# Attention by pairs of heads in the front of a two-layer model, with the front's steps dealt anew

## The chip, the core and the metric

The kernel runs on one NeuronCore of a Trainium2 chip. Its engines are TensorE (PE in the rows, with PEld for its weight loads), VectorE (DVE), ScalarE (ACT), GpSimd (POOL) and SyncE (SP), whose queue issues the DMAs. Each engine takes its own instructions in order; semaphores tie them together. The metric is the device time of one launch in microseconds.

## The reference, cut to what matters

One sequence of 256 tokens, 1024 channels, 16 heads of 64 channels. Layer 0 is a recurrent time mix and a dense feed-forward; layer 1 is attention and a mixture of eight experts. With one block of 256 keys the attention has no other blocks to select, so it is plain causal attention:

```python
q = _heads(x @ w_q).transpose(0, 2, 1, 3)
s_own = jnp.einsum('bhqd,bhkd->bhqk', q_c, k_own).astype(jnp.float32) * scale
s_own = jnp.where(k_pos[None, :] <= q_pos[:, None], s_own, -jnp.inf)
p = jax.nn.softmax(jnp.concatenate([s_sel, s_own], axis=-1), axis=-1)
o = ... + jnp.einsum('bhqk,bhkd->bhqd', p_own.astype(v_own.dtype), v_own)
return (o @ w_o).astype(x.dtype)
...
logits = (x @ router).astype(jnp.float32)
top_logits, top_idx = lax.top_k(logits, TOP_K_EXPERTS)
for e in range(N_EXPERTS):
    out = out + gates[..., e:e + 1] * swiglu(x, w_gate[e], w_up[e], w_down[e])
```

## The kernel before

The program has two parts. `front` does everything up to the router: the projections of the time mix, its chunked scan in four units (two halves of the channels by two tiles of 128 tokens), the output projection, the dense feed-forward, the projections to keys, queries and values, attention, its output projection and the choice of experts. `moe` then streams the weights of the eight experts from HBM, 2 MB at a time, through nine places in SBUF, and multiplies them with the tokens gathered for each expert.

Inside `front` the work is written as generators ("chains"), each a row of steps that ends at a `yield`. A string of letters, `ORDER`, says which chain makes its next step; the instructions land on their engines' queues in exactly that order, for PE, DVE, ACT, POOL and SP alike. Chains `a` to `d` are the units of the scan, `v` is `project_out` (values, keys and queries, then the output projection), `h`, `i`, `j`, `k` are four attention chains, `n` is `heads_out`, and `A` fetches expert weights ahead.

Weights of `front` arrive as 1 MB raw blocks. ACT casts each half block to a rounded high part (line 287) and DVE subtracts it to get a low part (line 288); a product is then three matmuls, high by high, high by low, low by high (lines 317 to 319; 1075 to 1078 for keys and queries).

Attention before takes one head at a time. `heads(i)` makes the heads 4·grp + i. Queries and keys lie with channels on partitions, two heads to a tile, so a head is one half of the 128 rows. Per head PE makes the scores of query tile 0 against key tile 0 (line 1134, 128 columns) and of query tile 1 against both key tiles (line 1136, 256 columns), each with a stationary side of 64 rows, and after each adds the causal mask by a 128-column bf16 matmul with an identity (lines 1135, 1137). An fp32 matmul is two instructions in the trace. DVE takes the row maxima (1140 to 1142), ACT the exponentials with their sums (1145). PE transposes the three 128x128 pieces of P (1150), DVE copies them out for even heads and ACT for odd ones (1153), and PE multiplies with the transposed P as the stationary side and 64 columns of values moving (1157 to 1159). `heads_out` takes four heads at a time: it divides by the sums (1169, 1171), transposes the result to channel-major with four PE transposes (1181) and splits it into high and low for the output projection. The PSUM tag `sc` has six banks, `mm` two.

Of the kernel before, what the change touches and what calls it, by code (L numbers as in the profile page):

```python
# [21 lines left out]
N = 64  # L22
# [159 lines left out]
def load_ln(g, i):  # L182
# [16 lines left out]
    "pXPmPXPXPmPPmpPXmmPpppppPpmppmpsppmPpspsPpppPssppmpPspPspppmPsPmppppGpppmmppmppvpmPGGPpPppXmmPGGmGPp"  # L199
    "mmpppPpmpPpGPGppspGmGaaaPasaOPsapaappPGOGOppppsPpspppppOapPbpObaaOpsaappaGOpaapbPpaPaappaaeasPppabaP"  # L200
    "basbbObpPpaaOappaGbaPpObapaabdpapbaadbpbbbpEddppabadPPpOdEcbbOEbapbEbaOdEdbbcddpcbddcdpbdddppccbpdEb"
    "dpdpbbpdcbcbpbbsdaadbabdcdbaadbabbdbbcbcdbbcdEccddbddeEdeeEeeeEldeecEeceEeEceeccEeeEEecddeeecEeeEcde"
    "edcdEccdceeccedeccdccceeceedcecEedEecedcecELemEccEeeceeccecLLedLeLcleLLlllLlLlllLlLlllllLllLLlllllll"
    "llLLelLLleLllllllLlllllllLlLllLlElLLlllllLLLlLLlalLlLlLlllllLlLlllcLLllLllLlllLLlLLllllllLlLLLllLLll"
    "LLlLLllllLLlllllllLlLlLllLLLlOLLllLllLLlllllllLllLlLLllLllLllLlLLllllllLlllLLlLlllllllLlLLlllLlLLlll"
    "LllllLLLlllLLlllllLLlLLLlllLlllLLlllLLLlLlLlLLLlblLLLWlllllLllWyyllyylWyyylyllyWWWyyyllWllzLWxvzvvzv"
    "zzvzzvzvzvzzvzvvvWvWvvWAvvWvvWWvvWWvvvWvyvWvvvWvWWWWvvvhkiWhAWhPjkvvvvAvWjWvivjhikhjiWjkkWWAkvnvWzWv"
    "AWhvvvvvijhkijnhhWjjikAjAWkkiWiWjWvvhinvvrvvvWvkhjknihhhiWnWikhkjAvijWvvWvWvkjihWWnijknvrvnvvvnvvWWv"
    "fvvvGuvvvAfvkffdvfAvfWfvivgvfruguAfgAArwuugwgugwjwAuuwgwftwwgtugggxfAqqAtqhwtqqqtAttxA"
# [24 lines left out]
def front(es, g, split, zH, zL, res):  # L234
# [774 lines left out]
    qT, kT, V, oT, av, sums = {}, {}, {}, {}, {}, {}  # L1009
# [30 lines left out]
    def project_out():  # L1040
# [51 lines left out]
        for j in range(2):  # L1092
            for kc in range(4):
                yield from W.need(kc * 512)
                yield "o%d" % (kc // 2)
                for tt in range(NT):
                    oH, oL = oT[0]
                    product(po[tt, j], oH[:, kc, tsl(tt)], oL[:, kc, tsl(tt)], *W.cols(kc * 512, 512), kc == 0, False)
                yield
        ws = {}  # L1100
        for tt in range(NT):
            for j in range(2):
                for kc in range(4):
# [5 lines left out]
                    yield "o%d" % (2 + kc // 2)  # L1109
# [8 lines left out]
    def heads(i):  # L1118

        for grp in range(4):  # L1120
            h = 4 * grp + i
            hp, s = divmod(h, 2)
            j, c = divmod(hp, 4)
            if i == 0:
                yield "at"
                av[grp] = bank("sc", (128, NT, 4, N))
                sums[grp] = g.small.tile([128, NT, 4], F32, name="sums", tag="sums")
                steps.post("av%d" % grp)
            yield "av%d" % grp
# [9 lines left out]
            st = g.small.tile([128, 4], F32, name="ast", tag="ast", bufs=4)  # L1139
            nc.vector.tensor_reduce(st[:, 0:1], sc[:, 0:128], AX, OP.max)  # L1140
            nc.vector.tensor_reduce(st[:, 1:2], sc[:, 128:384], AX, OP.max)
            nc.vector.tensor_scalar(st[:, 2:4], st[:, 0:2], -0.125, None, op0=OP.mult)
            P_ = att("P", (128, 384), 4)
            for tt, cs in enumerate((slice(0, 128), slice(128, 384))):
                nc.scalar.activation(P_[:, cs], sc[:, cs], AF.Exp, bias=st[:, 2 + tt:3 + tt], scale=0.125,
                                     accum_out=sums[grp][:, tt, i:i + 1])
            yield
            pt = bank("sc", (128, 384))
            for n in range(3):
                nc.tensor.transpose(pt[:, n * 128:(n + 1) * 128], P_[:, n * 128:(n + 1) * 128], g.ident)  # L1150
            PT = att("PT", (128, 384), 4)
# [4 lines left out]
            hs = slice(h % 8 * N, h % 8 * N + N)  # L1156
# [3 lines left out]
            steps.post("av%d.%d" % (grp, i))  # L1160
            yield

    def heads_out():

        for grp in range(4):
            for i in range(4):
                yield "av%d.%d" % (grp, i)
# [691 lines left out]
```

## Time and profile before

| | us |
|---|---|
| median of 3 runs | 1445.87 (1444.23 to 1451.18) |
| the profiled execution | 1449.14 |
| its span, first to last instruction | 1447.3 |
| first matmul on expert weights | 612.88 |
| PE busy over the span | 1338.2 (92%) |
| DVE busy | 779.7 (54%) |
| ACT busy | 380.8 (26%) |

The rows below come from the profiled execution. A window row gives, for a stretch of the span, how long each engine was busy (instructions in brackets), the clock that TensorE was granted (1.00 is 2.4 GHz, 0.50 is 1.2 GHz), the share of time that the 16 DMA engines were busy, and GB/s. A timeline row gives start, duration, engine, line, operation, out<-in and shapes; since matmuls overlap, the time that one costs its engine is the distance to the next row's start, not its duration.

### The profile page before, as it was taken

What the parts mean: (1) busy time and instruction counts of PE and PEld (TensorE: products, weight loads), DVE (VectorE), ACT (ScalarE), POOL (GpSimd) and SP (SyncE); (2) the same over time, 40 slices, a digit from 0 to 9 for tenths busy, and PEclk for the clock granted to TensorE, in tenths of its full rate; (3) what the DMA queues carried; (4) which work ended last, traced back from release to release, by engine and by line L of the source; (5) the groups of instructions that cost most, each with busy time, mean ns of one, the idle gap of its engine ahead of it and who ended that gap; (6) DMA issues with size and microseconds to landing.
All of it is one profiled execution on the core that took longest, in us unless ns stands there. A gap on an engine that the chain in (4) does not pass through costs nothing. (4 is left out here: it accounts for less than half of the span.)

```text
span 1447.3 us, 25902 instructions
## 1 busy us (share of the span) xinstructions
PE 1338.2 (92%) x10935; PEld 756.1 (52%) x10935; DVE 779.7 (54%) x1884; ACT 380.8 (26%) x678; POOL 10.4 (1%) x32
## 2 busy tenths in 40 slices
PE   7999998899999999899987999997999999998874
PEld 5776876678878987733332334332443343332221
DVE  8777888664558344744643433543432433544445
ACT  5666655453433343301110100110100110100100
POOL 1000000000000000000000000000000000000000
PEclk9999999999999988799999999999999999999997
DMA  6533153565554553779999999999999999999993
GB/s 219 207 134 107 37 188 135 179 241 188 204 204 164 214 204 118 291 310 425 423 425 424 422 426 425 423 424 422 425 426 423 425 400 406 403 425 421 424 425 159
DMA packets 49876, 446.58 MB, mean 309 GB/s; under 512 B 5792, under 2 KB 5920, under 8 KB 11840
## 3 DMA queue, kind: packets, MB, share of 16 engines
q1 hardware_dynamic: 49728, 444.42, 76.0%
q8 instruction: 115, 1.88, 0.5%
q14 instruction: 33, 0.27, 0.1%
HBM read 443.35 MB, written 1.05 MB: 307 GB/s over the span
## 5 line engine op out<-in xcount | busy, mean ns | idle before, releaser
L1460 PE MATMUL gu<-raw,x 128*64 128x512 f32 x1216 | 279.1, 604 | 27.4 <-DMA raw<-wm 22.8
L1498 DVE STREAM_TRANSPOSE t<-s 32x64 f32<-32x64 f32 (+1 forms) x896 | 241.4, 269 | 15.3
L288 DVE TENSOR_TENSOR w<-raw,w 128x1024 fp32r<-128x1024 f32 x140 | 168.2, 1221 | 87.5 <-ACT w L287 87.0
L1471 PE MATMUL y<-raw,t 128*64 128x512 f32 x880 | 200.7, 594 | 11.8 <-DMA raw<-wm 11.8
L1483 DVE TENSOR_TENSOR s<-s,gu 64x512 f32<-64x512 f32 x56 | 38.0, 679 | 298.7 <-ACT s L1482 298.7
L1460 PEld LDWEIGHTS gu<-raw,x 128*64 128x64 f32 x1216 | 88.8, 138 | 196.9 <-issue 154.8
L287 ACT CAST w<-raw 128x1024 fp32r<-128x1024 f32 x140 | 144.2, 1050 | 94.4 <-DMA raw<-wd 44.1
L1460 PE MATMUL gu<-half,x 128*64 128x512 f32 x576 | 134.9, 615 | 12.9 <-DMA half<-wm 9.7
L1471 PEld LDWEIGHTS y<-raw,t 128*64 128x64 f32 x880 | 65.6, 137 | 133.7 <-issue 125.3
L1482 ACT ACTIVATE s<-gu 64x512 f32<-64x512 f32 x56 | 33.2, 593 | 370.0 <-PE gu L1460 370.0
L1460 PEld LDWEIGHTS gu<-half,x 128*64 128x64 f32 x576 | 42.9, 141 | 94.1 <-issue 85.8
L1489 ACT ACTIVATE s<-gx 64x256 f32<-64x256 f32 x56 | 21.0, 375 | 266.9 <-PE gx L1465 144.8
L1490 DVE TENSOR_TENSOR s<-s,gx 64x256 f32<-64x256 f32 x56 | 23.8, 425 | 103.5 <-ACT s L1489 102.0
L317 PE MATMUL sc<-w,h 128*128 128x512 f32 (+1 forms) x176 | 66.8, 380 | 0.0
L318 PE MATMUL sc<-w,h 128*128 128x512 f32 (+1 forms) x176 | 66.5, 378 | 0.1
L319 PE MATMUL sc<-w,l 128*128 128x512 f32 (+1 forms) x176 | 66.1, 375 | 0.0
L1465 PE MATMUL gx<-raw,x 128*32 128x256 f32 x832 | 47.6, 380 | 1.1 <-DVE t L1498 1.1
L1465 PEld LDWEIGHTS gx<-raw,x 128*32 128x32 f32 x832 | 26.1, 110 | 27.0 <-issue 11.7
L1477 PE MATMUL yx<-raw,t 128*32 128x256 f32 x672 | 40.2, 379 | 0.0
L318 PEld LDWEIGHTS sc<-w,h 128*128 128x128 f32 x176 | 33.3, 189 | 7.2 <-DVE w L288 0.8
L317 PEld LDWEIGHTS sc<-w,h 128*128 128x128 f32 x176 | 33.3, 189 | 6.5
L319 PEld LDWEIGHTS sc<-w,l 128*128 128x128 f32 x176 | 33.3, 189 | 6.5
(405 smaller groups left out, 1903.3 us busy)
## 6 DMA issues: line engine op xcount, KB each, us to landing
raw<-wm SPq DMA_DIRECT2D x112, 2048.0 KB, 24.6
half<-wm SPq DMA_DIRECT2D x74, 1024.0 KB, 24.5
raw<-wd SPq DMA_DIRECT2D x72, 1024.0 KB, 4.9
raw<-wm SPq DMA_DIRECT2D x38, 1024.0 KB, 30.8
vec<-vecs SPq DMA_DIRECT2D x20, 256.0 KB, 5.6
ln<-vecs SPq DMA_DIRECT2D x8, 512.0 KB, 7.0
x<-xT SPq DMA_DIRECT2D x4, 256.0 KB, 5.6
raw<-wd SPq DMA_DIRECT2D x2, 512.0 KB, 5.4
```

What stands on the lines that cost most here:

```text
L287: nc.scalar.copy(wh, raws[n - 1][:, cs])
L288: nc.vector.tensor_sub(wl, raws[n - 1][:, cs], f32(wh))
L317: nc.tensor.matmul(o, ah, bh, start=start, stop=False)
L318: nc.tensor.matmul(o, ah, bl, start=False, stop=False)
L319: nc.tensor.matmul(o, al, bh, start=False, stop=stop)
L1460: nc.tensor.matmul(a.pg[64 * m:64 * m + 64], a.x[:, kc, 0:MAIN], w[m], start=kc == 0, stop=kc == KC - 1)
L1465: nc.tensor.matmul(a.px[32 * q:32 * q + 32], a.x[:, kc, MAIN:CAP], w[q // 2][:, q % 2 * 256:q % 2 * 256 + 256], start=kc == 0, stop=kc == ...
L1471: nc.tensor.matmul(a.y[64 * n:64 * n + 64], a.t[:, kt, 0:MAIN], w[:, n * 512:n * 512 + 512], start=a.j == 0 and kt == 0, stop=a.j == NJ - ...
L1477: nc.tensor.matmul(a.yx[32 * q:32 * q + 32], a.t[:, kt, MAIN:CAP], w[:, q * 256:q * 256 + 256], start=a.j == 0 and kt == 0, stop=a.j == NJ ...
L1482: nc.scalar.activation(a.s[0:64], a.pg[64:128], AF.Silu)
L1483: nc.vector.tensor_mul(a.s[0:64], a.s[0:64], a.pg[0:64])
L1498: nc.vector.transpose(a.t[32 * b:32 * b + 32, k:k + n // 128, c:c + 32], src[:, b])
```

## The change

Attention is made by pairs of heads. A chain makes the pairs `i` and `4 + i`; a pair is one whole tile of queries and keys. Its two heads get a PSUM bank each for their scores. A bf16 matmul of 384 columns first writes the mask into each bank; then the two heads' score matmuls follow in turn, one on the upper 64 rows of the array, the other on the lower 64. DVE divides P by its sums before the transposes (a reciprocal and four multiplications by a column for each pair). All copies of the transposed P are ACT's. The second product has the values as the stationary side, 64 columns for each head, and the transposed P moving (256 columns for key tile 0, 128 for key tile 1); its two heads write the two halves of one bank's partitions, channel-major already, so `heads_out` and its transposes are gone and each pair is split by itself. The output projection waits for each pair instead of each four heads. `ORDER` is a new string for the whole of `front`. The expert part is the same.

```diff
-                yield "o%d" % (kc // 2)
+                yield "o%d" % kc
...
-                    yield "o%d" % (2 + kc // 2)
+                    yield "o%d" % (4 + kc)
...
-        for grp in range(4):
-            h = 4 * grp + i
-            hp, s = divmod(h, 2)
+        for hp in (i, 4 + i):
             j, c = divmod(hp, 4)
...
-            q_, k_ = qT[j][HF[s], c], kT[j][HF[s], c]
-            sc = bank("sc", (128, 384))
-            nc.tensor.matmul(sc[:, 0:128], q_[:, 0:128], k_[:, 0:128], start=True, stop=False)
-            nc.tensor.matmul(sc[:, 0:128], g.identb, g.cmask, start=False, stop=True)
-            nc.tensor.matmul(sc[:, 128:384], q_[:, 128:256], k_, start=True, stop=False, skip_group_check=True)
-            nc.tensor.matmul(sc[:, 256:384], g.identb, g.cmask, start=False, stop=True, skip_group_check=True)
+            q_, k_ = (t[j][:, c] for t in (qT, kT))
+            sc = [bank("sc", (128, 384)) for _ in range(2)]
+            for s in range(2):
+                nc.tensor.matmul(sc[s], g.identb, g.cmask, start=True, stop=True)
+            for cs, qs, ks in ((slice(0, 128), slice(0, 128), slice(0, 128)), (slice(128, 384), slice(128, 256), slice(0, 256))):
+                for s in range(2):
+                    nc.tensor.matmul(sc[s][:, cs], q_[HF[s], qs], k_[HF[s], ks], start=False, stop=True,
+                                     skip_group_check=True)
...
+            nc.vector.reciprocal(st[:, 0], st[:, 2])
+            for s in range(2):
+                for tt, cs in enumerate(cols):
+                    nc.vector.tensor_scalar(P_[s][:, cs], P_[s][:, cs], st[:, 0, s, tt:tt + 1], None, op0=OP.mult)
...
-            eng = nc.scalar.copy if s else nc.vector.tensor_copy
-            eng(PT, pt)
+                nc.scalar.copy(PT[s], pt)
...
-            nc.tensor.matmul(av[grp][:, 0, i], PT[:, 0:128], V[j][:, 0, hs], start=True, stop=True)
-            nc.tensor.matmul(av[grp][:, 1, i], PT[:, 128:256], V[j][:, 0, hs], start=True, stop=False)
-            nc.tensor.matmul(av[grp][:, 1, i], PT[:, 256:384], V[j][:, 1, hs], start=False, stop=True)
+            av = bank("sc", (128, 256))
+            for kt, qs, ps in ((0, slice(0, 256), slice(0, 256)), (1, slice(128, 256), slice(256, 384))):
+                for s in range(2):
+                    v_ = V[j][:, kt, (2 * c + s) * N:(2 * c + s) * N + N]
+                    nc.tensor.matmul(av[HF[s], qs], v_, PT[s][:, ps], start=kt == 0, stop=True, skip_group_check=True)
...
-            rs = g.small.tile([128, NT, 4], F32, name="rs", tag="rs")
-            nc.vector.reciprocal(rs, sums[grp])
-            o = att("o", (128, NT, 4, N), 2)
-            nc.vector.tensor_mul(o, av[grp], rs[:, :, :, None].to_broadcast([128, NT, 4, N]))
...
-            for c in range(2):
-                for tt in range(NT):
-                    nc.tensor.transpose(p[:, c, tt], o[:, tt, 2 * c:2 * c + 2].rearrange("p h n -> p (h n)"), g.ident)
-            split_to(nc, *(t[:, c] for t in oT[grp // 2]), p.rearrange("p c t n -> p c (t n)"))
+            split_to(nc, *(t[:, c] for t in oT[j]), av)
```

Of the table of letters, the end (attention and router) before and now:

```diff
-    "AWhvvvvvijhkijnhhWjjikAjAWkkiWiWjWvvhinvvrvvvWvkhjknihhhiWnWikhkjAvijWvvWvWvkjihWWnijknvrvnvvvnvvWWv"
+    "vvjWrWWAivWvvkiikjikkjkvWvjvkjvvkvrkWWWkjkhivvjWikAhWihhkAWWvvWvvvviAWhhivhiijhiAiWvjvvjvWvfvvvvfffh"
```

PE in the middle of attention, where one head's scores are followed by another head's second product. Before:

```order
L1134 MATMUL sc<-K,Q 128x128
L1135 LDWEIGHTS identb
L1135 MATMUL sc<-cmask,identb 128x128
L1136 MATMUL sc<-K,Q 128x256
L1137 LDWEIGHTS identb
L1137 MATMUL sc<-cmask,identb 128x128
L1157 MATMUL sc<-V,PT 128x64
L1158 MATMUL sc<-V,PT 128x64
L1159 MATMUL sc<-V,PT 128x64
```

Now, the transposes of two pairs, then a pair's masks and scores, then a pair's second product:

```order
L1158 MATMUL sc<-ident,P 128x128 x12
L1129 LDWEIGHTS identb
L1129 MATMUL sc<-cmask,identb 128x384
L1129 LDWEIGHTS identb
L1129 MATMUL sc<-cmask,identb 128x384
L1132 MATMUL sc<-K,Q 128x128 x2
L1132 MATMUL sc<-K,Q 128x256 x2
L1167 MATMUL sc<-PT,V 64x256 x2
L1167 MATMUL sc<-PT,V 64x128 x2
```

The masks moved ahead of the scores, the two heads of a pair stand side by side, and the second product has 64 output partitions with 256 or 128 columns for each instruction.

PE at the end of attention, before the last output projections; `oH` is the high part of the attention's output, `w` the projection's weights. Before:

```order
L1150 MATMUL sc<-ident,P 128x128 x9
L1157 MATMUL sc<-V,PT 128x64
L1158 MATMUL sc<-V,PT 128x64
L1159 MATMUL sc<-V,PT 128x64
L1181 MATMUL sc<-ident,o 128x128 x4
L1157 MATMUL sc<-V,PT 128x64
```

Now:

```order
L1158 MATMUL sc<-ident,P 128x128 x6
L317 MATMUL mm<-w,oH 128x512
L318 MATMUL mm<-w,oH 128x512
L319 MATMUL mm<-w,oL 128x512
L317 MATMUL sc<-w,oH 128x512
L318 MATMUL sc<-w,oH 128x512
L319 MATMUL sc<-w,oL 128x512
L1167 MATMUL sc<-PT,V 64x256 x2
L1167 MATMUL sc<-PT,V 64x128 x2
L1158 MATMUL sc<-ident,P 128x128 x6
L1167 MATMUL sc<-PT,V 64x256 x2
L1167 MATMUL sc<-PT,V 64x128 x2
```

Six projection matmuls now stand between one pair's transposes and its second product, and a second product of another pair behind the last transposes.

ACT in the scan stage, where sigmoid (463, 481) and exponential (511, 528) need different tables. Before:

```order
L526 ACTIVATE X<-GK 128x512
L528 ACT_TABLE_LOAD
L528 ACTIVATE AR<-AR 128x512
L529 ACTIVATE GK<-sc 128x512
L530 ACTIVATE AR<-sc 128x512
L583 COPY bT<-sc 128x512
L105 CAST zH<-xm 128x512
L583 COPY bT<-sc 128x512
L511 ACTIVATE pch<-sc 128x4x2
L463 ACT_TABLE_LOAD
L463 ACTIVATE h<-sc 128x512
```

Now:

```order
L583 COPY bT<-sc 128x512 x2
L511 ACT_TABLE_LOAD
L511 ACTIVATE pch<-sc 128x4x2
L481 ACT_TABLE_LOAD
L481 ACTIVATE sg<-sc 128x160
L287 CAST w<-raw 128x1024 x2
L486 COPY sgA<-sc 128x128
L487 COPY sgB<-sc 32x128
L526 ACTIVATE X<-GK 128x512
L528 ACT_TABLE_LOAD
```

The sigmoids moved between exponentials; over the whole program there are twelve table loads instead of ten.

## Rows read from the trace of the kernel before

**Rows 1.** The page, 40 slices: TensorE's granted clock in tenths.

```profile
PEclk9999999999999988799999999999999999999997
```

**Rows 2.** Windows by stage: PE, PEld, DVE, ACT, POOL busy; clock, DMA share, GB/s.

```profile
72.00:288.00 216.00, 196.36 (x4073) 154.56 (x4072) 168.90 (x329) 122.87 (x227) 2.15 (x3) 0.96 0.37 129
...
464.00:592.00 128.00, 128.00 (x771) 108.35 (x770) 62.09 (x121) 49.19 (x109) 0.00 (x0) 0.89 0.50 191
...
612.00:628.00 16.00, 14.96 (x60) 5.39 (x62) 6.74 (x25) 3.36 (x5) 0.00 (x0) 0.83 0.42 158
628.00:1180.00 552.00, 520.60 (x3574) 203.52 (x3572) 239.45 (x747) 56.76 (x127) 0.00 (x0) 1.00 1.01 423
1180.00:1260.00 80.00, 79.44 (x672) 31.37 (x670) 32.92 (x104) 8.19 (x18) 0.00 (x0) 1.00 0.97 395
```

**Rows 3.** Timeline of PE: start, us, engine; the first matmuls on expert weights.

```profile
612.88 5.39 PE L1460 MATMUL gu<-raw,x 128*64 128x512 f32 x14 [0.97 <-ACT x L1348]
```

**Rows 4.** Timeline of PE: one head's scores and second product, full clock.

```profile
510.48 0.48 PE L1134 MATMUL sc<-K,Q 64*128 64x128 f32 x2
510.90 0.23 PE L1135 MATMUL sc<-cmask,identb 128*128 128x128 bf16 x1
511.06 0.70 PE L1136 MATMUL sc<-K,Q 64*128 64x256 f32 x2
511.69 0.23 PE L1137 MATMUL sc<-cmask,identb 128*128 128x128 bf16 x1
511.75 0.39 PE L1157 MATMUL sc<-V,PT 128*128 128x64 f32 x2
...
512.51 0.48 PE L1134 MATMUL sc<-K,Q 64*128 64x128 f32 x2
```

**Rows 5.** Timeline of PE: the same of another head at half clock.

```profile
534.20 0.79 PE L1134 MATMUL sc<-K,Q 64*128 64x128 f32 x2
...
536.37 0.64 PE L1157 MATMUL sc<-V,PT 128*128 128x64 f32 x2
...
537.79 0.79 PE L1134 MATMUL sc<-K,Q 64*128 64x128 f32 x2
```

**Rows 6.** Windows as in Rows 2: the stretches of half clock within attention.

```profile
491.00:498.00 7.00, 7.00 (x28) 5.27 (x28) 3.08 (x8) 3.85 (x14) 0.00 (x0) 0.51 0.43 157
...
532.00:542.00 10.00, 10.00 (x36) 7.34 (x36) 4.33 (x10) 4.09 (x11) 0.00 (x0) 0.50 0.31 108
...
559.50:569.00 9.50, 9.50 (x27) 6.14 (x26) 6.50 (x15) 4.97 (x15) 0.00 (x0) 0.50 0.32 113
```

**Rows 7.** Timeline of PE: tiles on two row halves (L759), two column halves (L1460).

```profile
212.41 0.68 PE L759 MATMUL sc<-D,FQ 64*64 64x64 f32 x16
212.93 0.75 PE L642 MATMUL sc<-P,LT 64*64 64x64 f32 x30
...
1413.28 3.65 PE L1460 MATMUL gu<-raw,x 128*64 128x512 f32 x16 [1.09 <-DMA raw<-wm]
1416.76 0.60 PE L1471 MATMUL y<-raw,t 128*64 128x512 f32 x2
```

**Rows 8.** Timeline of PE: four transposes of the attention's output, full clock.

```profile
575.13 0.60 PE L1181 MATMUL sc<-ident,o 128*128 128x128 f32 x4
575.58 0.33 PE L1157 MATMUL sc<-V,PT 128*128 128x64 f32 x2
```

**Rows 9.** Groups by line and shape: count, busy us, mean ns, idle before.

```profile
L1153 DVE COPY PT<-sc 128x384 f32<-128x384 f32 x8 | 4.4, 554 | 6.8 <-PE sc L1150 6.8
L1153 ACT COPY PT<-sc 128x384 f32<-128x384 f32 x8 | 3.7, 481 | 9.4 <-PE sc L1150 9.4
L1171 DVE TENSOR_TENSOR o<-sc,rs 128x512 f32<-128x512 f32 x4 | 2.8, 692 | 0.3
L1145 ACT ACT_TABLE_LOAD x1 | 1.3, 1283 | 2.2 <-DVE ast L1142 2.2
...
L1373 DVE TENSOR_SCALAR G<-slots,pos,sel 128x96 fp32r<-128x96 f32 x16 | 4.6, 327 | 0.3
```

**Rows 10.** Waits of PE up to 440 us: us in total, times, longest.

```profile
PE sc L871 <- DVE h L154: 5.3, 2, 4.9
```

More of the change, by code (lines that the diff above doesn't have):

```diff
@@ L1008, in front @@
     at = []
-    qT, kT, V, oT, av, sums = {}, {}, {}, {}, {}, {}
+    qT, kT, V, oT = {}, {}, {}, {}
     def rooms():
@@ L1163, in heads_out @@
[L1163 to L1167, printed above, removed]
-            rs = g.small.tile([128, NT, 4], F32, name="rs", tag="rs")
-            nc.vector.reciprocal(rs, sums[grp])
-            o = att("o", (128, NT, 4, N), 2)
-            nc.vector.tensor_mul(o, av[grp], rs[:, :, :, None].to_broadcast([128, NT, 4, N]))
-            yield
-            if grp == 0:
+            q_, k_ = (t[j][:, c] for t in (qT, kT))
+            sc = [bank("sc", (128, 384)) for _ in range(2)]
@@ new lines, in heads @@
+            for s in range(2):
[4 more added lines that the diff above has]
+                                     skip_group_check=True)
+            yield
+            st = g.small.tile([128, 3, 2, NT], F32, name="ast", tag="ast", bufs=4)
@@ new lines, in heads @@
+            cols = (slice(0, 128), slice(128, 384))
+            for s in range(2):
+                for tt, cs in enumerate(cols):
+                    nc.vector.tensor_reduce(st[:, 0, s, tt:tt + 1], sc[s][:, cs], AX, OP.max)
+            nc.vector.tensor_scalar(st[:, 1], st[:, 0], -0.125, None, op0=OP.mult)
+            yield
+            P_ = [att("P", (128, 384), 4) for _ in range(2)]
+            for s in range(2):
+                for tt, cs in enumerate(cols):
+                    nc.scalar.activation(P_[s][:, cs], sc[s][:, cs], AF.Exp, bias=st[:, 1, s, tt:tt + 1], scale=0.125,
+                                         accum_out=st[:, 2, s, tt:tt + 1])
@@ new lines, in heads @@
+            yield
+            nc.vector.reciprocal(st[:, 0], st[:, 2])
+            for s in range(2):
+                for tt, cs in enumerate(cols):
+                    nc.vector.tensor_scalar(P_[s][:, cs], P_[s][:, cs], st[:, 0, s, tt:tt + 1], None, op0=OP.mult)
+            yield
+            PT = []
+            for s in range(2):
+                pt = bank("sc", (128, 384))
+                for n in range(3):
+                    nc.tensor.transpose(pt[:, n * 128:(n + 1) * 128], P_[s][:, n * 128:(n + 1) * 128], g.ident)
+                PT.append(att("PT", (128, 384), 4))
+                nc.scalar.copy(PT[s], pt)
+                yield
@@ L1174, in heads_out @@
+            yield "V%d" % j
+            av = bank("sc", (128, 256))
+            for kt, qs, ps in ((0, slice(0, 256), slice(0, 256)), (1, slice(128, 256), slice(256, 384))):
+                for s in range(2):
+                    v_ = V[j][:, kt, (2 * c + s) * N:(2 * c + s) * N + N]
+                    nc.tensor.matmul(av[HF[s], qs], v_, PT[s][:, ps], start=kt == 0, stop=True, skip_group_check=True)
+            yield
+            if hp == 0:
                 oT[0] = [at[0].tile([128, 4, 256], F32R, name=n, tag=n) for n in ("oH", "oL")]
-            if grp == 2:
+                steps.post("oT")
@@ L1355, in front @@
                         e=early(), l=late(), y=norm_turn(0), z=norm_turn(1), x=rooms(), A=ahead(),
-                        v=project_out(), h=heads(0), i=heads(1), j=heads(2), k=heads(3), n=heads_out(), f=router(0), u=choose(0), w=choose(1),
+                        v=project_out(), h=heads(0), i=heads(1), j=heads(2), k=heads(3), f=router(0), u=choose(0), w=choose(1),
                         g=router(1), t=tokens(), q=weights(), r=weigh())
@@ L1732, in trunk @@
     nc.gpsimd.iota(ij, pattern=[[1, 128]], base=0, channel_multiplier=-1, allow_small_or_imprecise_dtypes=True)
-    g.cmask = c.tile([128, 128], BF16, name="cmask")
-    nc.gpsimd.tensor_scalar(g.cmask, ij, 0.0, -1e30, op0=OP.is_gt, op1=OP.mult)
+    g.cmask = c.tile([128, 384], BF16, name="cmask")
+    nc.gpsimd.memset(g.cmask[:, 128:256], 0.0)
+    for i in (0, 256):
+        nc.gpsimd.tensor_scalar(g.cmask[:, i:i + 128], ij, 0.0, -1e30, op0=OP.is_gt, op1=OP.mult)
     g.tri = cs.tile([128, 128], F32, name="tri")
```

47 lines of the change are left out of this document (14 added, 33 removed).

## The prediction

> **What bounds the kernel now.** I read the windows by stage first. From 628 us on the DMA engines are busy all the time at 423 GB/s [rows 2]: the expert part waits for its weights, and its length does not depend on what is done before it. Between 612 and 628 us the DMA share is only 0.42: the nine places are full, and no new block is fetched until the first expert matmuls, at 612.88 us [rows 3], give a place back. So the stream starts when PE reaches the expert part, and each microsecond by which `front` ends earlier should end the launch a microsecond earlier. The one stretch in the expert part where DMA falls below that (395 GB/s, PE busy 79.44 of 80) is counted from the same start and moves with it [rows 2].
>
> In `front` I look for the engine that sets the pace. From 464 to 592 us, keys, queries, values and attention, PE is busy 128.00 of 128 us, DVE 62.09 and ACT 49.19 [rows 2]: PE sets the end there, and a microsecond of PE work taken away is a microsecond gained. From 72 to 288 us, the scan, PE is busy 196.36 of 216 and DVE 168.90: PE waits 19.6 us in all, on chains through DVE, the longest for 4.9 us [rows 2, 10]. The granted clock dips three times within attention, for 7.0, 10.0 and 9.5 us [rows 6], where the page's slices show only a shallow dip [rows 1], and PE is busy throughout, so these dips lie on the path.
>
> **The change, part by part.** Prices of one head at full clock, as distances of starts [rows 4]: 128-column scores 0.42, mask 0.16, 256-column scores 0.63, mask 0.06, together 1.27; second product 0.76. An fp32 matmul is two instructions, so 128 more columns cost 0.105 per instruction, or 0.82 ns a column, and what is left of the 0.21 per 128-column instruction is 0.105 of weight load that nothing hides.
>
> *Scores.* A pair costs 2.54 us before. Now: two masks of 384 columns at three times 0.06, 0.36, and the 0.10 by which a mask ahead of a 64-row load is longer (0.16 against 0.06), 0.46. The scores are 2.10 if the two heads run one after the other. Two tiles on different halves of the rows do run side by side in the scan: 16 instructions of 64 columns take 0.52, 32 ns each [rows 7], where 64 columns alone would be 52: a factor of 1.6. With it the scores are 1.31, the pair 1.77, and eight pairs save 6.2 us. Bounds: one after the other, 2.56, a loss of 0.2; side by side with the loads hidden too, 384 columns by two instructions by 0.82 ns = 0.63, the pair 1.09, a gain of 11.6. I take 6.2, because the row shows overlap but with smaller tiles.
>
> *Second product.* 1.52 a pair before. Now each head streams 384 columns in two instructions, 0.63. Two column halves overlap in the expert part: 16 instructions of 512 columns take 3.48, 218 ns each [rows 7], where 420 would be due alone: 1.9. So 1.26/1.9 = 0.66, and 0.21 for the second half's start one 256-column instruction later, 0.87; eight pairs save 5.2. Bounds: no overlap and every load exposed (8 by 0.105), 2.10, a loss of 4.6; 0.66 alone, a gain of 6.9.
>
> Switches between whole rows and halves show in the rows as the 0.10 above. The Trainium skill (TensorEngine Tiling (Array Packing), Key Properties) says that changing the tiling mode drains TensorE. By that the change adds two switches a pair around the column halves, 16 by 0.10 = 1.6 us, and the whole gain below would be 17.5 instead of 19.1.
>
> *Output transposes.* Sixteen go, at 0.45 for four [rows 8]: 1.8 us, with nothing in their place.
>
> *Clock.* At half clock a head's scores take 2.17 and its second product 1.42 [rows 5], 1.7 and 1.9 times the full-clock prices; at 1.8 the 26.5 us of half clock [rows 6] would have been 14.7: 11.8 us are to be had. The falls lie in attention, whose scores before used 64 rows at a time, with half of a 128-column instruction being load [rows 4 to 6]. Now both halves work, the score time shrinks by a third, and whole-array masks stand in it. No row shows the new mixture. I take two of the three falls as gone, 7.9 us; bounds 11.8, and one fall more, minus 3.9.
>
> *New waits.* In the new order the first scores follow the query matmuls directly, so they wait for the copies of queries, and at the end of attention a pair's second product stands soon behind its transposes and waits for ACT's two copies (0.48 each [rows 9]); what is queued behind on PE is the output projection. Other pairs' work and six projection matmuls stand in between at most places. I take 2 us; bounds 0 and, every pair paying both copies, 7.7.
>
> *DVE and ACT.* DVE gains four multiplications a pair. The nearest row is 327 ns for 96 columns; with 1.35 ns a column from the 692 ns for 512 [rows 9], 0.33 for 128 and 0.50 for 256, 1.66 a pair, 13.3 in all; it loses 2.8 (the division in `heads_out`) and 4.4 (copies) [rows 9]: 68 us in a stage of some 109. ACT gains eight copies, 3.8, to 53. Both are hidden by PE as long as their queues don't hold it up; if that cover goes, rival 2 is the price. Two more table loads in the scan, 1.3 us each [rows 9], fall on ACT, busy 122.87 of 216 there [rows 2]: nothing. The expert blocks fetched ahead are moved among the weight blocks of SP's queue; DMA is half idle there (0.50 [rows 2]), so nothing.
>
> *The order of the rest.* The same instructions stand ahead of attention as before, dealt anew among the four units. PE's 19.6 us of waiting in the scan could shrink or grow; I take 0, with 5 us (the longest wait, 4.9 [rows 10]) to either side.
>
> Sum: 6.2 + 5.2 + 1.8 = 13.2, + 7.9 − 2.0 = 19.1. Against the profiled execution, 1449.1, that is 1430.0; its time stands 3.3 above the median of the runs shown, so on the median's scale it is 1426.8.
>
> **The rivals.**
> 1. *The clock falls as before.* Long runs of transposes (twelve in a row) and scores may still bring it down. For it: no fall stands in products of whole tiles, and attention remains made of small ones. Against: row halves now work together. Gain 13.2 − 2.0 = 11.2: 1435.
> 2. *DVE and ACT become the bound in attention.* A pair's chain is now maxima, exponentials, division, transposes, copy, product, through three engines, and DVE also makes the low parts of the weights. If the two worked in turn, 68 + 53 = 121 us would take the place of 128: a gain of 7, 1439. Against: they need only overlap a little. The Trainium skill (TensorEngine Tiling (Array Packing), PSUM Bottleneck) warns of just this, that tiling speeds up TensorE but not what empties PSUM; the rows so far show PE waiting for neither.
> 3. *The halves don't run together.* Then only the transposes are won, and weight loads eat that: 1.8 − 0.2 − 4.6 = −3.0, with some clock regained about 0: 1446. Against it stand both factors of rows 7.
> 4. *Everything overlaps*, loads too, and no fall is left: 20.3 + 11.8 = 32: 1414.
> 5. *Slower: the scan in the new order.* There PE and DVE are both near full, and each step placed behind another unit's work on DVE's queue makes PE wait. It ends on the other side once it adds more than the 19.1 plus 7.2: six new waits like the longest, 4.9, are 29.4, +10: 1456. For it: the order is new everywhere. Against: all present waits there make 19.6.
>
> **How the numbers follow.** A measurement of this kernel tells about 0.5% (7.2 us) from no change. Forecast 0.50 (1419 to 1435), rival 1 0.17, rival 2 0.10, rival 3 0.08, rival 4 0.09, rival 5 0.06. Faster (below 1438.6): the forecast, 1, 4 and a part of 2, 0.79. The same: 3 and the rest of 2, 0.14. Slower: 5 and a little of 3, 0.07. The range 1411 to 1442 leaves out rivals 3 and 5 and little else; it is the sum with the order's 5 us, from rival 4 to rival 2. I predict 1427.
>
> **What would show it.** The first expert matmul should start near 594 us, and the time from there to the end stay at 834. The new score line should show about 1.3 us from its first to the next line's start, the second product 0.9, with PE still busy without gaps through attention; the half-clock windows there should fall from 26.5 us to below 10. Gaps of PE ended by ACT's copies or DVE's multiplications would speak for rival 2, a PE busy sum from 72 to 288 us unchanged with a longer stage for rival 5. The forecast is wrong if the expert stage's length changes, which would mean that the stream doesn't start with PE.

## The result: 1421.95 us, and the profile after

The changed kernel takes 1421.95 us (median of 4 runs, 1421.65 to 1422.70); the kernel before, beside it, 1446.04 (1444.23 to 1451.18). The ratio is 0.9829, with a 95% interval of 0.9803 to 0.9854: 24.1 us less. The forecast was 1427, its range 1411 to 1442; the direction holds, the time lies in the range, and the gain is 5 us larger than the sum gave.

The profiled execution of the changed kernel took 1422.70, with a span of 1420.9. Between four marks on PE (the first matmul of keys, the first transpose of the router, the first matmul on expert weights, the end) the two spans divide so:

| stretch | before | after | difference |
|---|---|---|---|
| to the first key matmul | 462.48 | 464.79 | +2.31 |
| keys, queries, values, attention, its projection | 125.17 | 97.20 | −27.97 |
| router, to the first expert matmul | 25.23 | 23.50 | −1.73 |
| experts, to the end | 834.39 | 835.45 | +1.06 |
| span | 1447.28 | 1420.94 | −26.33 |

The marks after, from the timeline of PE (start, us, engine, line, operation, out<-in, shape; idle before in brackets); the last answers to [rows 3]:

```profile
464.79 0.28 PE L1075 MATMUL mm<-zH,w 128*128 128x256 f32 x1
...
561.99 0.60 PE L1254 MATMUL sc<-ident,h 128*128 128x128 f32 x4
...
585.49 5.73 PE L1454 MATMUL gu<-raw,x 128*64 128x512 f32 x18 [1.24 <-ACT x L1342]
```

One pair of heads after, from the same view; it answers to [rows 4], which show one head:

```profile
520.24 0.49 PE L1129 MATMUL sc<-cmask,identb 128*128 128x384 bf16 x2
520.65 0.93 PE L1132 MATMUL sc<-K,Q 64*128 64x128 f32 x8
521.51 1.52 PE L1167 MATMUL sc<-PT,V 128*64 128x256 f32 x16
522.96 0.50 PE L1129 MATMUL sc<-cmask,identb 128*128 128x384 bf16 x2
```

Distances of starts: two masks 0.41, the scores of both heads 0.86, together 1.27, which is what one head cost before; the second product of two pairs 1.45, 0.73 a pair. The windows by stage after (PE, PEld, DVE, ACT, POOL busy; clock, DMA share, GB/s), which answer to [rows 2]; the second row is the router:

```profile
464.00:562.00 98.00, 98.00 (x708) 84.95 (x707) 60.23 (x130) 52.50 (x121) 0.00 (x0) 1.00 0.61 226
562.00:585.00 23.00, 19.04 (x106) 17.06 (x104) 19.76 (x73) 7.22 (x14) 0.00 (x0) 0.71 0.91 347
...
600.00:1152.00 552.00, 518.11 (x3564) 205.16 (x3562) 238.50 (x745) 56.28 (x126) 0.00 (x0) 1.00 1.01 423
...
72.00:288.00 216.00, 194.40 (x4075) 154.10 (x4075) 168.16 (x330) 124.07 (x230) 2.29 (x3) 0.97 0.38 129
```

In attention PE is busy 98.00 of 98 us, with DVE at 60.23 and ACT at 52.50, and the granted clock is 1.00 throughout: none of the three stretches of half clock [rows 6] is left. The expert part streams at 423 GB/s as before. In the scan PE now waits 21.6 us, 2.0 more than in the profiled execution before.

### The profile page after: what moved, and what is told of

Its sections match the earlier page's. It is cut to its first block, busy times and chain, and to the rows that moved or that the text cites. A ratio compares the mean times of both kernels' runs of the same rounds, so it can differ in the third digit from the quotient of the medians.

```text
span 1420.9 us, 25812 instructions
## 1 busy us (share of the span) xinstructions
PE 1306.1 (92%) x10871; PEld 733.1 (52%) x10871; DVE 779.2 (55%) x1904; ACT 385.4 (27%) x692; POOL 11.2 (1%) x34
## 3 DMA queue, kind: packets, MB, share of 16 engines
HBM read 443.35 MB, written 1.05 MB: 313 GB/s over the span
## 5 line engine op out<-in xcount | busy, mean ns | idle before, releaser
L1459 PEld LDWEIGHTS gx<-raw,x 128*32 128x32 f32 x832 | 26.1, 110 | 27.0 <-issue 11.7
L317 PE MATMUL mm<-w,xs 128*128 128x512 f32 x64 | 28.9, 452 | 8.5 <-ACT xs L105 8.5
```

The costliest lines, as they stand in the source:

```text
L317: nc.tensor.matmul(o, ah, bh, start=start, stop=False)
L1459: nc.tensor.matmul(a.px[32 * q:32 * q + 32], a.x[:, kc, MAIN:CAP], w[q // 2][:, q % 2 * 256:q % 2 * 256 + 256], start=kc == 0, stop=kc == ...
```

## The experiments

The table gives each kernel's median against the kernel before in the same runs (whose median moves between 1445.9 and 1448.65 from chip to chip), the length of the attention stretch in the trace (first key matmul to first router transpose), and the half clock inside it, counted from windows of 2 us.

| kernel | median | against before | attention stretch | half clock in it |
|---|---|---|---|---|
| before | 1446.04 | | 125.17 | 27, three falls |
| changed | 1421.95 | −24.1 | 97.20 | none |
| 1. old scores | 1436.01 | −9.9 | 111.88 | 7, one fall |
| 2. scores head by head, order alone | 1420.74 | −25.2 | 97.27 | none |
| 3. second product head by head, order alone | 1420.53 | −25.4 | 97.34 | none |
| 4. old second product, not turned back | 1422.73 | −23.2 | 101.57 | none |
| 5. old second product and transposes | 1428.62 | −19.6 | 105.37 | none |
| 6. mask between the heads | 1431.28 | −16.9 | 104.73 | none |
| 7. old masks, heads side by side | 1426.43 | −22.2 | 98.99 | none |
| 8. old scores and old second product | 1452.80 | +4.6 | 128.76 | 27, four falls |
| 9. before, with the mask ahead | 1437.72 | −10.5 | 113.19 | 3, one fall |
| 10. changed, old order ahead of attention | 1420.28 | −25.8 | 97.20 | none |
| 11. before, new order ahead of attention | 1452.67 | +6.6 | 125.20 | 27, three falls |
| 12. normalisation twice | 1421.93 | −24.1 | 97.21 | none |

My theory at the start of them: PE sets the pace of attention, so what PE saves there reaches the end unshortened; the scores save because two halves of the array's rows work side by side; the falls of the clock belong to the old form of the products. Rivals: DVE or ACT sets the pace (then PE's savings are worth less), the order of the products or the masks carry the gain, and the new order of the steps removed the falls.

### 1. The old scores put back

```diff
-for s in range(2): matmul(sc[s], g.identb, g.cmask, start=True, stop=True)
-for cs, qs, ks in (...):
-    for s in range(2): matmul(sc[s][:, cs], q_[HF[s], qs], k_[HF[s], ks], start=False, stop=True)
+for s in range(2):
+    q, k = q_[HF[s]], k_[HF[s]]
+    matmul(sc[s][:, 0:128], q[:, 0:128], k[:, 0:128], start=True, stop=False)
+    matmul(sc[s][:, 0:128], g.identb, g.cmask[:, 0:128], start=False, stop=True)
+    matmul(sc[s][:, 128:384], q[:, 128:256], k, start=True, stop=False)
+    matmul(sc[s][:, 256:384], g.identb, g.cmask[:, 256:384], start=False, stop=True)
```

> The changed kernel with the scores alone put back: each head of a pair again makes its 128 columns, a 128-column mask, its 256 columns and a mask, one head after the other. Theory A (the two row halves of the array work side by side, and this alone is worth 8 x (2.54 - 1.27) = 10.2 us at full clock, passed on to the end unshortened): 1432 us if the clock stays up, and the attention stretch about 108 us instead of 98. Theory B (the falls of the clock come from this old form of the scores): up to 12 us more, 1444. Rival (PE had slack elsewhere and the halves gain nothing): 1422, as without the edit.

Measured 1436.01 (ratio to before 0.9926, 0.9903 to 0.9950), 14.2 us of the gain gone. The attention stretch grows by 14.68 us and the span by 13.3: what PE loses here does reach the end, which also settles that the expert part moves with its start. The timeline of PE, one pair at full clock:

```profile
527.97 0.48 PE L1130 MATMUL sc<-K,Q 64*128 64x128 f32 x2
528.39 0.23 PE L1131 MATMUL sc<-cmask,identb 128*128 128x128 bf16 x1
528.55 0.70 PE L1132 MATMUL sc<-K,Q 64*128 64x256 f32 x2
529.17 0.23 PE L1133 MATMUL sc<-cmask,identb 128*128 128x128 bf16 x1
529.33 0.48 PE L1130 MATMUL sc<-K,Q 64*128 64x128 f32 x2
...
530.70 0.65 PE L1167 MATMUL sc<-PT,V 128*64 128x256 f32 x4
```

From 527.97 to 530.70 the pair takes 2.73 instead of 1.27. Eight times 1.46 is 11.7 us, more than the 10.2 of theory A: the mask behind a head's last scores takes 0.16 here, where it took 0.06 before [rows 4]. And the clock falls once, within the first six heads, which stand in a row from 486.80 us on, as the windows show (the first row is the fall, the second what stands ahead of it):

```profile
492.50:499.50 7.00, 7.00 (x26) 5.01 (x26) 2.98 (x9) 4.61 (x17) 0.00 (x0) 0.51 0.46 152
486.80:492.50 5.70, 5.70 (x26) 3.36 (x26) 3.21 (x9) 2.45 (x3) 0.00 (x0) 1.00 0.99 420
```

The other 3 of the 14.7 us are this fall. One of three falls came back: theory A holds, B by a part.

### 2 and 3. The order of the products within a pair

```diff
-for cs, qs, ks in (...):
-    for s in range(2):
+for s in range(2):
+    for cs, qs, ks in (...):
         matmul(sc[s][:, cs], q_[HF[s], qs], k_[HF[s], ks], ...)
```

and the same exchange of loops around the second product.

> The changed kernel with the four score products of a pair in another order: both of the first head, then both of the second, so that neighbouring products mostly use the same half of the rows; the masks stay ahead. Theory A1 (a half's products overlap only with neighbours of the other half, and a lone half shows its weight loads): a pair of score products 2.10 us instead of 0.86, 8 x 1.24 = 9.9 us more, 1432; if the boundary between the heads still overlaps, about 7 us, 1429. Theory A2 (the products run side by side whatever their order, or the gain lay in the masks): 1422.

> The changed kernel with the four second products of a pair in another order: both of the first head, then both of the second, so that neighbours mostly write the same half of the columns. Theory A1 (overlap only between neighbours on different halves): a pair 1.26 us without overlap and with loads hidden, up to 2.10 with all loads seen, instead of 0.73: 4.2 to 11 us more, 1426 to 1433. Theory A2 (order does not matter): 1422.

Measured 1420.74 and 1420.53: no loss. A1 falls. In the program of run 2 the products of a pair now stand as 128, 256 columns of the first head, then 128, 256 of the second. The trace has them otherwise. All instructions of line 1132 that start between 518.90 and 519.27 us (count, duration min/median/max in ns, first and last start, form):

```profile
L1132 PE MATMUL sc<-K,Q x4: 272/322/373, 519.0 to 519.2; 64*128 64x128 f32 x4
```

All four 128-column instructions, those of the second head too, start before any of the four of 256 columns, two by two within 13 or 14 ns, and the pair's scores take 0.87 in all:

```profile
518.95 0.93 PE L1132 MATMUL sc<-K,Q 64*128 64x128 f32 x8
519.82 1.52 PE L1167 MATMUL sc<-PT,V 128*64 128x256 f32 x16
```

So PE takes the second head's 128-column product ahead of the first head's 256-column product, which stands before it; who wants the overlap need not write the halves in turn. The Trainium skill (TensorEngine Tiling (Array Packing), Key Properties) says that different tiles load and multiply independently; the row agrees. So the statement in the first section that each engine takes its instructions in order does not hold between the halves of the rows.

Run 3 shows the same length for the column halves. From its start to the next line's, the second product of two pairs takes 1.50, 0.75 a pair, against 0.73 in the pair shown above:

```profile
503.44 1.57 PE L1167 MATMUL sc<-PT,V 128*64 128x256 f32 x16
504.94 0.39 PE L1075 MATMUL mm<-zH,w 128*128 128x256 f32 x1
```

### 4. The old second product alone

```diff
-for kt, qs, ps in ((0, slice(0, 256), slice(0, 256)), (1, slice(128, 256), slice(256, 384))):
-    for s in range(2): matmul(av[HF[s], qs], v_, PT[s][:, ps], ...)
+for s in range(2):
+    for kt, tt, ps in ((0, 0, slice(0, 128)), (0, 1, slice(128, 256)), (1, 1, slice(256, 384))):
+        matmul(av[:, tt * 128 + s * N:tt * 128 + s * N + N], PT[s][:, ps], v_, ...)
```

> The changed kernel with the second product alone in its old shape: six products a pair, the transposed probabilities stationary and 64 value columns moving. Their sums land token-major in the same bank and are not transposed, so the attention output is not the reference's. Theory A (the turned product is worth 8 x (1.52 - 0.73) = 6.3 us): 1428, with the clock up. Theory C (the falls of the clock come from these short 64-column products): up to 12 us more, 1440. Rival (the product was hidden behind DVE and ACT anyway): 1422.

Measured 1422.73. In attention PE's second product goes from 6.05 us to 10.67 (sums of distances of starts), the stretch from 97.20 to 101.57. But the time from the first expert matmul to the end is 832.35 instead of 835.45, since with other attention output the router chooses other tokens: that part has 4240 matmul instructions instead of 4912. Where the attention output differs, a time cannot be read across the router; only the stretch ahead of it can. That gives 4.4 to 4.6 us for the turned product, with the clock up: theory A holds with 4.6 in place of 6.3, and C falls.

### 5. The old second product with its transposes

```diff
+(as in 4) ; o = att("o", (128, 256), 2) ; nc.scalar.copy(o, av)
...
+p = bank("sc", (128, 256))
+for tt in range(NT): nc.tensor.transpose(p[:, tsl(tt)], o[:, tsl(tt)], g.ident)
-split_to(nc, *(t[:, c] for t in oT[j]), av)
+split_to(nc, *(t[:, c] for t in oT[j]), p)
```

> The changed kernel with the second product in its old shape and the transposes of its output put back (ACT copies the sums to a tile, PE turns them a step later), so that the attention output is the reference's again. Rigid theory (what PE loses in attention reaches the end unshortened): 10.67 - 6.05 = 4.6 us by the run with the old shape, and 8 x 0.21 = 1.7 for the transposes, 6.3: 1428. Rival (the run with the old shape alone ended only 1 us later because the part behind attention really became 3 us shorter by the shift): 3 us, 1425. If DVE or ACT set the pace now, the copy adds up to 8 x 0.4 = 3.2 us, 1431.

Measured 1428.62 (1426.67 to 1430.65), 4.6 us more by the comparison with before in the same runs, 6.7 by the medians. In the profiled execution, the slowest of the four, the stretch is 8.2 us longer: about 4.6 for the products, 1.5 for the transposes, and 1.6 in which PE waits for ACT's copy, this edit's own (us in total, times, longest); half a microsecond is left over:

```profile
PE sc L1182 <- ACT o L1170: 1.6, 3, 0.5
```

The forecast of 6.3 lies between. No fall of the clock.

### 6 and 7. What the scores' gain is made of

Run 6 puts each head's mask ahead of its own products, so that a whole-row product stands between the halves; run 7 keeps the halves together and puts the 128-column masks back behind the products.

```diff
 (6)
+for s in range(2):
+    matmul(sc[s], g.identb, g.cmask, ...)
+    for cs, qs, ks in (...): matmul(sc[s][:, cs], q_[HF[s], qs], k_[HF[s], ks], ...)
 (7)
+for cs, qs, ks, ms in (...):
+    for s in range(2): matmul(sc[s][:, cs], q_[HF[s], qs], k_[HF[s], ks], ...)
+    for s in range(2): matmul(sc[s][:, ms], g.identb, g.cmask[:, ms], ...)
```

> The changed kernel with one edit in the scores: mask and two products of the first head, then mask and two products of the second, so that a product of whole rows stands between the two halves. Theory A1' (the run with the heads' products in another order showed that each half of the rows takes its own work ahead, whatever the order, as long as nothing of whole rows stands between; this is what the gain of the scores rests on): a lone head's two score products took 1.03 us in the run with the scores put back, so a pair 2.06 instead of 0.86, 8 x 1.2 = 9.6 us more, 1431. Theory M (the gain lay in the masks: fewer changes between bf16 and fp32, or between whole and half rows): a pair has two changes instead of one, 8 x 0.1 = 0.8 us, 1422 to 1423.

> The changed kernel with the masks alone put back to where they were: the 128-column products of both heads, a 128-column mask for each, the 256-column products of both heads, a mask for each. The halves can still run side by side. This closes a square of four: masks ahead and side by side 1422, masks ahead and heads apart 1431.3, masks behind and heads apart 1436.0. Theory M (masks behind cost by breaking the scores up once more and at full clock only): the trace with the scores put back has a head at 1.36 us against 1.29 with the mask ahead of each head, so 16 x 0.1 to 16 x 0.25, 1424 to 1426, no fall of the clock. Theory B'' (masks behind the scores by themselves bring a fall of the clock in attention): about 3.5 us more, 1428 to 1430.

Measured 1431.28 and 1426.43; the attention stretch is 7.5 and 1.8 us longer. One pair in run 6, then one in run 7 (timeline of PE):

```profile
523.83 0.33 PE L1129 MATMUL sc<-cmask,identb 128*128 128x384 bf16 x1
524.08 0.92 PE L1131 MATMUL sc<-K,Q 64*128 64x128 f32 x4
524.93 0.34 PE L1129 MATMUL sc<-cmask,identb 128*128 128x384 bf16 x1
525.20 0.92 PE L1131 MATMUL sc<-K,Q 64*128 64x128 f32 x4
526.05 0.65 PE L1166 MATMUL sc<-PT,V 128*64 128x256 f32 x4
```

```profile
521.15 0.49 PE L1131 MATMUL sc<-K,Q 64*128 64x128 f32 x4
521.58 0.29 PE L1133 MATMUL sc<-cmask,identb 128*128 128x128 bf16 x2
521.79 0.70 PE L1131 MATMUL sc<-K,Q 64*128 64x256 f32 x4
522.43 0.28 PE L1133 MATMUL sc<-cmask,identb 128*128 128x128 bf16 x2
522.64 0.65 PE L1167 MATMUL sc<-PT,V 128*64 128x256 f32 x4
```

In run 6 one head's products take 0.85, as good as what both take side by side (0.86): the second head is free. A pair is 1.27 with masks ahead and heads together, 1.49 with masks behind, 2.22 with heads apart, 2.73 with both. Eight times 0.95 is the 7.6 us that the halves bring; moving the masks brings up to 0.2 a pair when the heads are together, up to 0.5 when apart (pairs that follow another pair's products have 1.37 and 2.61). With the masks behind, the halves bring 1.24 a pair instead of 0.95, so how the gain divides depends on which of the two is changed first. A1' holds, and M for its own smaller part; neither run has a fall of the clock (windows of run 6, then of run 7):

```profile
464.00:569.00 105.00, 105.00 (x705) 88.97 (x704) 60.04 (x130) 52.71 (x121) 0.00 (x0) 1.00 0.56 210
464.00:563.00 99.00, 98.93 (x720) 85.60 (x719) 59.58 (x129) 52.49 (x121) 0.00 (x0) 1.00 0.59 222
```

What stands between the halves in run 6 differs from them in two ways: it uses all rows, and it is bf16 with a weight load of its own. Which of the two ends the overlap was not separated.

### 8. Scores, second product and transposes all old, new order

The edits of 1 and 5 together.

> The changed kernel with scores, second product and output transposes all in their old form, in the new order of steps. At full clock 10.2 + 4.6 + 1.7 = 16.5 us more: 1438. Theory B (the falls of the clock hang on how much of attention is short products and masks, one fall of about 7 us having come back with the old scores): all three back, 26.5 us at half clock, so up to 12 us more, 1447 to 1451. Theory O (two of the three falls went with the new order of the steps, not with the products): one fall, 3.4 us, 1441 to 1442.

Measured 1452.80 (ratio 1.0030, 1.0013 to 1.0047): 28.7 us of the gain and more, where the two edits alone cost 14.2 and 4.6. The 10 us beyond their sum fit the clock: four falls stand in attention, 27 us of half clock where run 1 has 7 and run 5 none. At the prediction's factor of 1.8 the 20 us more are worth 9.

```profile
464.00:592.00 128.00, 126.38 (x764) 108.36 (x763) 59.66 (x128) 55.78 (x129) 0.00 (x0) 0.89 0.46 170
492.50:503.50 11.00, 11.00 (x45) 8.31 (x44) 3.11 (x9) 5.05 (x18) 0.00 (x0) 0.54 0.35 116
516.50:523.50 7.00, 7.00 (x36) 7.00 (x35) 2.41 (x6) 4.80 (x19) 0.00 (x0) 0.53 0.32 104
543.00:547.50 4.50, 4.50 (x14) 3.30 (x15) 4.40 (x18) 3.40 (x16) 0.00 (x0) 0.62 0.43 137
564.00:571.00 7.00, 6.48 (x21) 5.31 (x21) 4.09 (x13) 4.14 (x12) 0.00 (x0) 0.51 0.00 0
```

The mean clock of the stretch is 0.89, as before the change [rows 2]. So the new order does not change how much half clock there is; the shape of the products does. Theory B holds, 2 us above its range, and O falls.

### 9. The kernel before, with the mask ahead

```diff
-matmul(sc[:, 0:128], q_[:, 0:128], k_[:, 0:128], ...) ; mask of 128 ; matmul(sc[:, 128:384], ...) ; mask of 128
+matmul(sc, g.identb, g.cmask, start=True, stop=True)      # 384 columns
+matmul(sc[:, 0:128], q_[:, 0:128], k_[:, 0:128], ...) ; matmul(sc[:, 128:384], q_[:, 128:256], k_, ...)
```

> The kernel before with the mask alone changed: one product of 384 columns ahead of a head's scores instead of two of 128 behind each. Theory M (the loss of the old scores is in the changes between score and mask): 16 x (1.27 - 1.03 - 0.2) gives 16 x 0.04 to, if the first 128-column product then takes the 0.21 of an unbroken one, 16 x 0.2, 1 to 3 us less, 1443 to 1445, and the falls of the clock as before. Theory B' (the falls hang on the masks between the scores): up to 12 us less, 1433. Rival: no difference, 1446, since whole-row work still stands between any two heads.

Measured 1437.72 (1437.29 to 1437.89; ratio 0.9929, 0.9906 to 0.9952): 10.5 us faster. B' came nearest. The stretch is 12.0 us shorter, and the one fall left in it is short. It begins within the second row; ahead of it PE had waited 0.75 us for an exponential (the third row), and none of the falls of the kernel before has such a wait ahead of it:

```profile
463.00:576.00 113.00, 111.38 (x745) 96.66 (x744) 58.91 (x108) 49.79 (x109) 0.00 (x0) 0.98 0.56 208
492.00:498.00 6.00, 5.82 (x29) 4.72 (x30) 3.08 (x8) 3.45 (x12) 0.00 (x0) 0.72 0.37 124
492.05 0.89 PE L1149 MATMUL sc<-ident,P 128*128 128x128 f32 x3 [0.75 <-ACT P L1144]
```

At full clock the edit can give no more than 16 times 0.2 us; the larger part is the clock. Moving the mask in the old form buys over two fifths of what the whole change buys.

### 10 and 11. The order ahead of attention

Run 10 is the changed kernel with the first 793 letters of the old order and then the rest in the new order; run 11 is the kernel before with the first 789 letters of the new order.

> The changed kernel with the steps ahead of attention dealt in the order of the kernel before (its first 793 letters, then the rest in the new order). Theory O1 (the 2.3 us by which the first key product starts later after the change, 464.79 against 462.48, are a loss of the new order): 1419.7, and faster than both kernels. Rival (2 us there is the spread from one execution to the next: four runs with the new order started at 462.36 to 464.79): 1422, no difference, or slower where the rest of the new order doesn't fit behind the old front.

> The mirror image: the kernel before with the new order of the steps ahead of attention (its first 789 letters, then the rest in the old order). Theory O1: 1448.3, 2.3 us slower than the kernel before. Rival (spread): 1446.

Run 11 is 1452.67 (ratio 1.0042, 1.0019 to 1.0065), 6.6 us slower than before; its first key matmul starts at 466.28, 3.8 us later than before. Run 10 is 1420.28 (0.9818, 0.9782 to 0.9853), against the changed kernel's 0.9829 no difference that these runs can tell, though its first key matmul starts at 460.59, 4.2 us earlier than after the change. What it wins there, its profiled execution loses again in the expert part, 838.49 instead of 835.45. The clock dips there once (0.97 in the first row) and later DMA moves less (392 GB/s against 402 after), but the kernel before has such a dip too, in the third row, and its expert part is the shortest of those with the same routing, 834.39. So the cause of these 3 us stays open.

```profile
921.00:981.00 60.00, 49.75 (x219) 16.79 (x220) 22.37 (x74) 5.25 (x12) 0.00 (x0) 0.97 1.01 422
1101.00:1161.00 60.00, 59.48 (x530) 25.88 (x524) 27.01 (x81) 7.16 (x17) 0.00 (x0) 1.00 0.96 392
772.00:832.00 60.00, 51.85 (x344) 19.66 (x342) 26.70 (x81) 5.89 (x13) 0.00 (x0) 0.97 1.01 422
```

Nor is the loss ahead of attention shown. Part of run 11's 3.8 us stands where its two orders meet: there PE waits 3.2 us for DVE, where the kernel before waits 1.3 and the changed kernel has no such wait (waits of PE between 440 and 470 us: total, times, longest; run 11, then before):

```profile
PE mm L999 <- DVE h L154: 3.2, 1, 3.2
PE mm L999 <- DVE h L154: 1.3, 1, 1.3
```

And executions differ by as much as the orders do. With the old order ahead of attention the first key product starts at 460.59 (run 10), 462.48 (before) and 463.41 us (run 9); with the new one at 462.36 to 464.79 in ten kernels and at 466.28 in run 11. The means differ by 1.9 us, but the ranges overlap: a loss of about 2 us is likely, and the rival, spread, is not excluded. That undoing the new order is faster in the end is not shown either.

### 12. The normalisation twice

```diff
+extra = att("extra", (128, 384), 1)
+(four more tensor_scalar: extra <- P * 1/sum)
 nc.vector.tensor_scalar(P_[s][:, cs], P_[s][:, cs], st[:, 0, s, tt:tt + 1], None, op0=OP.mult)
```

> The changed kernel with the normalisation of the probabilities done twice, first into a spare tile that nobody reads: 32 more DVE instructions, 10.1 us by the trace of the changed kernel, in a stretch in which DVE is busy 60 of 98 us. Theory (PE sets the end and DVE has slack): 0 to 1 us, 1422 to 1423. Rival 2 (DVE or the chain of a pair through it sets the pace): up to 10 us, 1432.

Measured 1421.93, and a stretch of 97.21 us: nothing, with DVE at 67.02 us in the row instead of 60.23. DVE has the room, and a pair's longer chain holds up nobody. No run gave ACT more to do without a change on PE.

```profile
464.00:562.00 98.00, 98.00 (x709) 84.95 (x708) 67.02 (x166) 52.81 (x122) 0.00 (x0) 1.00 0.59 227
```

## Why the prediction was right, and where its terms were off

**The frame held.** The expert part stayed at 835.45 (834 forecast; 834.39 to 838.49 over all runs with the same routing), the first expert matmul came at 585.49 (594 forecast), and PE stayed without a gap in attention. Run 1 shows that the stretch passes on whole: it is 14.7 us longer and starts 1.2 earlier, and the span is 13.3 longer. The sizes were less good: of the 7 us by which the profiled gain exceeds the sum, the scores and the clock, both taken too small, make 7.5, and the smaller errors nearly cancel.

**Scores: forecast 6.2, measured 10.2**, 8 times (2.54 − 1.27). The mis-sized step is the price of the two heads apart and the factor on it. I took 2.10 for the products of a pair and divided by the 1.6 of the small scan tiles; run 6 shows 1.70 apart and 0.86 together, a factor of 2.0. The 0.105 of load "that nothing hides" per instruction was in part the price of the masks between the products: with the mask ahead, a lone head's products take 0.85 instead of 1.05. Counted with the masks ahead, 7.6 of the 10.2 are the halves and 2.6 the masks, where I had the masks at no gain. The upper bound, 11.6, was not reached, since a pair took 1.27 and not 1.09.

**Second product: forecast 5.2, measured 4.6.** The estimate of 0.87 was too high (0.73 in the pair shown, 6.05/8 = 0.76 on average), but so was the 1.52 for before: run 4 gives 10.67/8 = 1.33 for the old shape at full clock. Two errors that lean against each other. The Trainium skill's drain at a change of tiling mode (TensorEngine Tiling (Array Packing), Key Properties), 1.6 us by my estimate, is not shown here: the pair lies at most 0.1 above the 0.66 of full overlap without loads, 0.8 us in all. In the scores, run 7 has two more changes a pair and takes 0.1 to 0.2 longer, which would fit the estimate, but its masks also have other lengths and twice the weight loads, so the drain is not separated.

**Output transposes: forecast 1.8, measured 1.5 to 1.7**, by the transposes of run 5 and the 1.68 that left.

**Clock: forecast 7.9, measured about 11.4.** The stretch shrank by 27.97; 10.2 + 4.6 + 1.8 = 16.6 are full-clock work; 11.4 are left, next to the 11.8 that all three falls were worth by [rows 4 to 6]. I had guessed two of three falls. One argument for rival 1, that no fall stands in products of whole tiles, was read wrongly: the first fall begins among scores, but its half clock runs on through whole-tile key products, each 0.41 us long there instead of 0.28:

```profile
496.50 0.41 PE L1075 MATMUL mm<-zH,w 128*128 128x256 f32 x1
...
498.52 0.28 PE L1075 MATMUL mm<-zH,w 128*128 128x256 f32 x1
```

Runs 1, 5 and 8 show that no part alone brings all of them back: old scores alone one, old second product alone none, both four. Run 9 shows that in the old kernel the place of the masks was the larger part of it.

**New waits: forecast −2.0, measured 0.** PE waits for no copy and for no DVE result between 465 and 562 us; the covers that I named were enough.

**Order: forecast 0 ± 5, measured −2.3** in the two profiled executions, with 2.0 more waiting in the scan; by runs 9 to 11 this is no clearer than the spread of executions. So rival 5's mechanism is not shown, and its price, 29 us, is excluded. The router stage became 1.7 us shorter, which I had not counted; its half clock is 17 us instead of 20. It takes 23.5 to 23.6 us in every kernel with the new order behind attention, run 8 with all the old products too, and 24.1 to 25.2 with the old order, so the products' shape is not the cause; more was not tried.

**The sum.** 10.2 + 4.6 + 1.8 + 11.4 − 2.3 + 1.7 − 1.1 = 26.3 against the profiled execution (forecast 19.1), the clock being what the other terms leave, and 24.1 by the medians.

**The rivals.** 1 (clock as before) and 3 (halves not together) fall by the trace; 3 is what run 6 makes of the scores. 2 falls with run 12 for DVE, and for ACT by the trace alone, in which PE waits for no copy. What the Trainium skill warns of (TensorEngine Tiling (Array Packing), PSUM Bottleneck) does not show in this case: DVE and ACT are busy 60 and 53 of 98 us. My DVE estimate was high too, 13.3 us for the normalisation, although it took the 0.33 of 96 columns for 128; the groups after (count, busy us, mean ns of one, idle before) have 10.1:

```profile
L1152 DVE TENSOR_SCALAR P<-P,ast 128x256 f32<-128x256 f32 x16 | 5.6, 347 | 0.0
L1152 DVE TENSOR_SCALAR P<-P,ast 128x128 f32<-128x128 f32 x16 | 4.5, 284 | 0.3
```

Rival 4 was right in its clock part (no fall left) and came within 8 us.

**What stays open.** Which property of the mixture lets the clock fall. Heads apart do not by themselves (run 6 stays up), nor masks behind (run 7), nor 64-column products (run 5); old scores with masks between do, once, and with the old second product four times. Two things change together in these runs, how long PE spends on such work and how broken it is, and they were not separated.

## What to carry to other kernels

Two products on different halves of the array's rows cost what one costs (0.86 for a pair, 0.85 for a head alone), in both orders tried, as long as no product of whole rows stands between; so gather such pairs, and put the mask or bias that uses the whole array ahead of both. When small products sit in a stretch that PE bounds, look at the granted clock in narrow windows before pricing them: here it was worth as much as the products, it did not add up part by part, and in the old kernel moving the mask alone won most of it. And where a kernel's later part depends on the values (a router), an experiment that changes them is read only up to that point.

## What the runs showed of the hardware that I had not expected

- PE started the other row half's 128-column product 13 ns after the first head's, ahead of a 256-column product that stood before it in the program (run 2).
- A mask of whole rows between the halves (384 columns, 0.25 us) costs far more than itself: it takes the overlap, 0.95 a pair (run 6).
- The clock's price is not additive: edits that cost 14.2 and 4.6 us alone cost 28.7 together (runs 1, 5, 8).
- In the old kernel, moving the mask ahead of a head's scores took the half clock within attention from 27 us to 3 (run 9).
